# A static decoder-trunk kernel: four first units side by side, zeros on PE at the start, past's loads in a new order, an output projection in three parts, and new costs in the planner

## The chip, the cores and the metric

One core of a Trainium2 chip. The metric is the device time of one execution in microseconds (us); lower is better. The kernel of before took 3124.43 us (median of 3 runs).

## What is computed

One step of a two-layer hybrid decoder for a prompt of 256 rows and a sample group of 8 sequences of 4 rows (288 rows in all), width 2048, in fp32. Cut to what matters here:

```python
for layer in range(2):
    xn = rmsnorm(x, g_mix)
    if layer == 0:                                  # even mixer, phase "m0"
        u, v, q, kvc, kvs, kvw, gl = split(xn @ w_in)
        a = gelu(u) * spatial_gate(rmsnorm(gelu(v)))          # gMLP half
        # NSA half: rows of the past come through a page table (2048 rows per sequence)
        kc, vc = compress(past_cmp ++ new)          # blocks of 64 rows, weighted sums
        o_c, p = cmp_attend(q, kc, vc)              # p ranks the blocks: the 16 best are selected
        o_s = sel_attend(q, top16(p), past_sel ++ new)
        o_w = window_attend(q, past_win ++ new)
        x = x + concat(a, gates(gl) . (o_c, o_s, o_w)) @ w_out
    else:                                           # odd mixer (Mamba-2 SSD), phase "m1"
        x = x + ssd(conv(xn @ w_in), state) @ w_out
    x = x + conv_ffn(rmsnorm(x, g_ffn))             # phases "f0", "f1"
```

Every matrix product `xn @ w` is a projection below. Its weights come from HBM once: 860 tiles of 512 KB.

## The kernel before

**Projections.** TensorE (PE) spends most of its time on them. A unit is 128 output columns over 16 chunks (other counts for some kinds) of 128 inputs. For fp32 accuracy the input is held as `xh + xl` and a weight block as `whi + wlo`; a block of 128x128 is three matmuls with 288 columns: `xh,whi`, `xl,whi`, `xh,wlo` (in the rows: `acc<-xh,whi` and so on). So there are 860 x 8 x 3 = 20,640 projection matmuls. Weights arrive as `wraw` (8 blocks, 5 buffers); a piece is 4 blocks (12 matmuls on PE), for which ScalarE (ACT) writes `whi` (a cast, 128x512) and VectorE (DVE) `wlo` (a subtraction, 128x512), four pieces ahead of PE (`convert`). Positions in the program are counted in pieces below: at 0.1333 us per matmul a piece is 1.6 us of PE. Phase m0 has 212 pieces.

**Order.** All of it is static and fixed when the program is built. `body` walks `all_slots()`, one block after another, and between blocks steps side jobs: Python generators (norms, attention, SSD, loads) that each yield an operation. Whether an operation is put into the program at this point is decided by a planner, `Clock` and `Op`: a cost per engine and element, a hop of 0.2 us between engines, and for PE a margin. A PE operation of a side job is issued when the planner holds its inputs for finished; PE runs in order, so where the real producer is later than planned, PE stands still.

**Start.** `body` issues the input x as four DMAs of four chunks each, weights between them, then page tables and masks (in `enter_m0`). `make_x` writes `xh` (ACT) and `xl` (DVE) of all 16 chunks ahead of the first slot, GpSimd (POOL) squares and adds the even chunks, ACT and DVE the odd ones (`squares`). `make_rstd` sums the squares on PE (`sums`), forms `rstd` on DVE and ACT, and spreads it over the partitions with matmuls on `hl` and `rb`; the first units' results are scaled with it (`h<-acc,rstd`). The first four units (query heads) run one after another, so unit 0 needs all 16 chunks of x within its 16 blocks.

**Past.** `loads` fills a ring `st` of six 512 KB tiles: 64 tiles of compressed rows (`in_ccmp`, gathers by POOL), 8 + 8 of the window (`in_cwk`, `in_cwv`), 32 of selected keys (`in_cselk`; in turn a POOL gather, and four page DMAs on SyncE's queue) and 32 of selected values (`in_cselv`, gathers). `weigh` and `pool_blocks` turn the first 64 into compressed blocks (ACT and DVE weigh, PE sums); `sample` waits for them (flag `pooled`), for the queries and for the gates, then attends: compressed, window, selection of blocks (`rank`), selected keys (`ps<-st,qzr`) and values (`po<-st,PT`).

**Output projection of m0.** `EPARTS` splits its 16 inputs into two parts, chunks 0 to 5 and 6 to 15. Its last unit of part 0 asks for the sample group's attention output (flag `sample`, in `post_e`). With 16 x 10 blocks behind it, that point is piece 172 of 212. `evac_eo` adds a unit's sum of each part to `h`.

All operations of the engines pass one line of the recording layer, L379 in the rows (L391 after the change).

Of the kernel before, what the change touches and what calls it, by code (L numbers as in the profile page):

```python
# [2 lines left out]

# [16 lines left out]
KD = D // 128  # L20
# [5 lines left out]
PIECE, RAW, AHEAD = 4, 8, 4  # L26
EPS = 1e-6
SI, SCV, SH, SG = 4096, 6144, 64, 8
EPARTS = ((0, 6), (6, 16))
# [117 lines left out]
for _n, _w in (("rsel", 256), ("gm", 128), ("cdiag", 128), ("causal", 256), ("newm", 64), ("cadd", 8), ("c01", 8),  # L147
               ("winm", 4), ("vzm", 8), ("hm", 8), ("hmask", 2), ("tle", 128), ("ble", 32), ("i32", 32)):
    EMATS[_n] = (sum(w for _, w in EMATS.values()), _w)
# [4 lines left out]
def even_mats():  # L154
# [19 lines left out]
        i32=np.broadcast_to(t, (128, 32)),  # L174
# [136 lines left out]
class Clock:  # L311


    COST = {"vector": (0.07, 1.04e-3), "scalar": (0.1, 0.834e-3), "gpsimd": (0.147, 2.1e-3)}
    SLOW = {"reciprocal": 6.3e-3, "tensor_tensor_reduce": 0.7e-3}
    TABLES = {AF.Sqrt: 1, AF.Silu: 2, AF.Exp: 3, AF.Tanh: 3}
    HOP = 0.2

    def __init__(self):
        self.free = dict.fromkeys(("tensor", "vector", "scalar", "gpsimd", "sync"), 0.0)  # L320
# [30 lines left out]
class Op:  # L351
# [11 lines left out]
    def start(self):  # L363
# [12 lines left out]
    def run(self):  # L376
# [17 lines left out]
        elif eng == "tensor":  # L394
            n, m = c.width(self.outs[0]), c.width(self.ins[0])
            if self.name == "transpose":
                us = 0.109
# [7 lines left out]
        else:  # L405
# [4 lines left out]
            if eng == "scalar":  # L410
                c0 += 0.05 * ws.count(1)
# [3 lines left out]
            c.free[eng] = end = t + c0 + max(ws) * c.SLOW.get(self.name, c1)  # L415
# [88 lines left out]
class Trunk:  # L504
# [113 lines left out]
    def load_w(self, i):  # L618
        t = yield self.wraw.want([128, RAW, 128], F32, name="wraw")
        self.keep(t)  # L620
        yield self.off.sync.dma_start(t, self.I["w"][i])
# [34 lines left out]
    def body(self):  # L656
# [33 lines left out]
        self.sqs = [self.ssq, self.rstd]  # L690
# [4 lines left out]
        for n in range(KD):  # L695
            self.make_x(n, PHASES[0], n % 2 == 0)
            if n % 4 == 3 and n < AHEAD * PIECE // 2:
                for j in range(n // 4 * AHEAD // 2, (n // 4 + 1) * AHEAD // 2):
                    self.convert(j)
        self.job(self.squares(range(1, KD, 2)), 20.0)  # L700
# [3 lines left out]
        for si, (u, n) in enumerate(slots):  # L704
# [4 lines left out]
            if o == 0:  # L709
                self.convert(j + AHEAD)  # L710
            if n == 0:
# [3 lines left out]
                if free > 2 and (len(u.ks) < 8 or len(pending) >= PMAIN):  # L715
# [74 lines left out]
    def squares(self, ns):  # L790

        nc = self.off
        for i, n in enumerate(ns):
            sq = self.spare[i] if i else self.rstd
            yield nc.scalar.activation(sq, self.h[:, n], AF.Square)
        for i, n in enumerate(ns):
            if i:
                yield nc.vector.tensor_tensor(self.rstd, self.rstd, self.spare[i], op=OP.add)
            self.nsq += 1

    def make_rstd(self):
        nc = self.off
        while self.nsq < KD or self.si < 24:
# [601 lines left out]
    def enter_m0(self, l):  # L1405
# [11 lines left out]
        for n in ("iot", "ptc", "pts", "ptv"):  # L1417
            nc.sync.dma_start(getattr(self, n), I[n])
# [35 lines left out]
        nc.sync.dma_start(self.early, I["emat"][:, :EARLY])  # L1454
# [31 lines left out]
    def even_consts(self):  # L1486

        nc = self.off
        for t, n, c in ((self.ptc, 64, 1), (self.pts, 128, 0), (self.ptv, 32, 2)):
# [278 lines left out]
    def evac_uv(self, u):  # L1768
        nc = self.nc
        if u.half and u.g >= 4:  # L1770
            self.require(("n", u.g - 4 - u.g % 2))
        x = self.w4.tile([128, T], F32, name="x1") if u.half else self.y[:, u.g]
# [70 lines left out]
    def loads(self):  # L1843
# [20 lines left out]
        while self.si < 12:  # L1864
            yield 0.3
        for G in range(2):
            for j in range(8):
                for b in range(4 * G, 4 * G + 4):
                    t = yield from tile()
                    yield gat(t, I["ccmp"], self.ptc[:, 8 * b + j:8 * b + j + 1])  # L1870
                    self.got.append(t)
# [34 lines left out]
    def weigh(self, l, src, dst):  # L1906
# [5 lines left out]
        slots = [x[:, 512 * i:512 * i + 512] for x, n in ((y, 4), (self.S, 3), (self.Sw, 1)) for i in range(n)]  # L1912
        for i in range(64):
            while not src:
                yield 0.3
            t = src.popleft()
            yield [t]
            for h in range(2):
# [3 lines left out]
                else:  # L1922
                    yield nc.vector.scalar_tensor_tensor(slots[i % 8][:, 256 * h:256 * h + 256], a, self.wpq[:, h, 0:1], b,
                                                         op0=OP.mult, op1=OP.add)
            if not l:
                self.rel(t)
                t = slots[i % 8]
            dst.append(t)

    def pool_blocks(self, src):  # L1930

        nc = self.off
        for G in range(2):
            ps = yield self.pside.want([128, 512], F32, name="ps")
            for j in range(8):
                while len(src) < 4:
                    yield 0.3
                yield Burst([self.mm(ps[32 * b:32 * b + 32], self.wpt[:, 28 - 4 * j:60 - 4 * j], src.popleft(),
                                     start=(j == 0), stop=(j == 7)) for b in range(4)])
            yield nc.scalar.copy(self.acc[:, G].rearrange("p h c -> p (h c)"), ps)  # L1940
# [32 lines left out]
    def sample_cmp(self):  # L1973
        nc = self.off
        kct = self.S[:, 256:768].rearrange("p (G h r) -> p G h r", G=2, h=2)
# [45 lines left out]
    def rank(self):  # L2021

        nc = self.off
        v3 = lambda t: t.rearrange("p (n m) -> p n m", n=32)
        a, b = self.S[:, 0:1024], self.S[:, 1024:2048]
        i32 = self.E("i32")
        for G in range(2):
            i_m = self.imp[:, G, None, :].to_broadcast([128, 32, 32])
            i_n = self.imp[:, G, :, None].to_broadcast([128, 32, 32])
            yield nc.vector.tensor_tensor(v3(a), i32[:, :, None].to_broadcast([128, 32, 32]),  # L2030
                                          i32[:, None, :].to_broadcast([128, 32, 32]), op=OP.is_gt)
            yield nc.vector.tensor_tensor(v3(b), i_m, i_n, op=OP.is_equal)
            yield nc.vector.tensor_tensor(b, b, a, op=OP.mult)
            yield nc.vector.tensor_tensor(v3(a), i_m, i_n, op=OP.is_gt)
# [140 lines left out]
```

## Time and profile before

| what | us |
|---|---|
| runs: median, lowest, highest of 3 | 3124.43, 3123.25, 3126.43 |
| the profiled execution's own time | 3120.15 |
| its span, first to last instruction | 3118.4 |
| mean granted TensorE clock | 0.995 |
| PE busy | 3054.7 (98%) |

The rows come from one profiled execution: its span is 1.75 us shorter than its own time, and that time 4.28 us shorter than the median of the runs. PE is busy nearly throughout, so the rows that matter are those of the stretches where it is not, and those where its granted clock (the column PEclk, 1.00 is 2.4 GHz) is below 1. Waits are given with what ended them.

### The profile page before, as it was taken

How to read it: one execution, taken by the hardware profiler on the slowest of the kernel's cores; microseconds unless marked ns; L12 is line 12 of the kernel's file. 1: busy time of each engine (PE TensorE's matmuls, PEld its weight loads, DVE VectorE, ACT ScalarE, POOL GpSimd, SP SyncE). 2: the span in 40 equal slices, each digit the busy share in tenths (PEclk: the TensorE clock that was granted, in tenths of full speed). 3: DMA queues.
4: the chain of work that ended last, by engine and by line, in shares of the span. 5: the costliest groups of instructions: out<-in, count | busy, mean ns of one | idle time of the engine just before them, and what ended most of it. 6: DMA issues, size and time to landing. Idle time of an engine off the chain costs nothing.

```text
span 3118.4 us, 63001 instructions
## 1 busy us (share of the span) xinstructions
PE 3054.7 (98%) x23529; PEld 2953.2 (95%) x23529; DVE 2220.0 (71%) x4575; ACT 1614.9 (52%) x3227; POOL 661.2 (21%) x1044
## 2 busy tenths in 40 slices
PE   7999989999999999999999999999999999999999
PEld 7998879999999999999889988899999999999999
DVE  7987646776577567678889989875677646765764
ACT  6775634554455445555555555554455535544553
POOL 6434443000000000122444445430220000000000
PEclk9999999999999999999999999999999999999999
DMA  7987774444444444555455545565454444444454
GB/s 291 330 314 245 273 271 171 167 163 167 164 164 168 163 164 168 181 187 180 174 184 192 183 161 180 175 208 177 151 176 167 163 167 165 164 168 163 164 179 146
DMA packets 189187, 587.43 MB, mean 188 GB/s; under 512 B 23217, under 2 KB 42961, under 8 KB 188881
## 3 DMA queue, kind: packets, MB, share of 16 engines
q1 hardware_dynamic: 169680, 516.29, 47.7%
q0 software_dynamic: 19200, 67.12, 6.2%
q8 instruction: 185, 3.03, 0.4%
q14 instruction: 122, 0.99, 0.1%
HBM read 555.54 MB, written 27.78 MB: 187 GB/s over the span
## 4 chain that ended last, share of the span: by engine, by line
PE 85%; DVE 6%; DMA 3%; issue 2%; POOL 2%; ACT 2%; SPq 0%; DVEq 0%; ACTq 0%; POOLq 0%
PE acc L379 77%; PE ps L379 7%; DVE wlo L379 2%; DVE cv L379 1%; PE po L379 1%; DMA h<-in_h 1%; DVE h L379 1%; DMA st<-in_cselk,pts 1%; DMA st<-in_cselv,ptv 1%; ACT whi L379 1%; POOL ssq L379 1%; POOL nrm L379 0%; DMA wraw<-in_w 0%; DVE zt L379 0%; DVE cx L379 0%
## 5 line engine op out<-in xcount | busy, mean ns | idle before, releaser
L379 DVE TENSOR_TENSOR wlo<-wraw,whi 128x512 fp32r<-128x512 f32 x1720 | 1232.4, 720 | 781.5 <-ACT whi L379 778.5
L379 ACT CAST whi<-wraw 128x512 fp32r<-128x512 f32 x1720 | 1058.8, 620 | 1090.1 <-PE acc L379 872.7
L379 PE MATMUL acc<-xh,whi 128*128 128x288 f32 x5238 | 1577.2, 301 | 9.4 <-ACT whi L379 8.0
L379 PE MATMUL acc<-xl,whi 128*128 128x288 f32 x5238 | 1549.5, 296 | 3.2 <-DVE xl L379 3.1
L379 PE MATMUL acc<-xh,wlo 128*128 128x288 f32 x5238 | 1544.0, 295 | 1.3 <-DVE wlo L379 1.3
L379 PEld LDWEIGHTS acc<-xh,whi 128*128 128x128 f32 x5238 | 985.9, 188 | 30.0 <-issue 14.2
L379 PEld LDWEIGHTS acc<-xl,whi 128*128 128x128 f32 x5238 | 987.3, 188 | 10.4 <-DVE xl L379 4.8
L379 PEld LDWEIGHTS acc<-xh,wlo 128*128 128x128 f32 x5238 | 989.3, 189 | 1.7 <-DVE wlo L379 1.7
L379 PE MATMUL acc<-hidh,whi 128*128 128x288 f32 x1380 | 407.9, 296 | 0.0
L379 PE MATMUL acc<-hidl,whi 128*128 128x288 f32 x1380 | 407.1, 295 | 0.0
L379 PE MATMUL acc<-hidh,wlo 128*128 128x288 f32 x1380 | 406.1, 294 | 0.0
L379 POOL COPY fcv<-hx 128x18 f32<-128x18 f32 x176 | 36.6, 208 | 1439.8 <-DVE hx L379 1439.8
L379 PEld LDWEIGHTS acc<-hidh,wlo 128*128 128x128 f32 x1380 | 259.8, 188 | 0.0
L379 PEld LDWEIGHTS acc<-hidl,whi 128*128 128x128 f32 x1380 | 259.1, 188 | 0.0
L379 PEld LDWEIGHTS acc<-hidh,whi 128*128 128x128 f32 x1380 | 258.6, 187 | 0.0
L379 DVE SCALAR_TENSOR_TENSOR cv<-hx,prm,cv 128x304 f32<-128x304 f32 x352 | 187.1, 532 | 6.3
L379 DVE SCALAR_TENSOR_TENSOR cv<-cx,sw,cv 128x312 f32<-128x312 f32 x144 | 112.3, 780 | 6.6 <-ACT cv L379 3.2
L379 ACT ACTIVATE cv<-hx,prm 128x304 f32<-128x304 f32 x176 | 112.7, 642 | 0.0
L379 POOL DMA_INDIRECT st<-in_ccmp,ptc x64 | 84.4, 1319 | 94.6 <-DVE S L379 18.1
L379 DVE TENSOR_TENSOR hx<-acc,rstd 128x256 f32<-128x256 f32 x348 | 89.7, 301 | 0.2
L379 POOL TENSOR_TENSOR h<-h,ets 128x512 f32<-128x512 f32 x64 | 78.5, 1250 | 7.4 <-PE po L379 7.3
L379 POOL TENSOR_TENSOR ssq<-ssq,nrm 128x288 f32<-128x288 f32 x76 | 76.3, 1004 | 5.7
(347 smaller groups left out, 2673.3 us busy)
## 6 DMA issues: line engine op xcount, KB each, us to landing
wraw<-in_w SPq DMA_DIRECT2D x860, 512.0 KB
h<-in_h SPq DMA_DIRECT2D x64, 256.0 KB
out_h<-h SPq DMA_DIRECT2D x64, 256.0 KB
st<-in_cselk SPq DMA_DIRECT2D x64, 128.0 KB
st<-in_cwk POOLq DMA_DIRECT2D x8, 512.0 KB, 6.4
st<-in_cwv POOLq DMA_DIRECT2D x8, 512.0 KB, 4.9
h<-in_xT SPq DMA_DIRECT2D x4, 576.0 KB
h<-in_xT SPq DMA_DIRECT2D x16, 144.0 KB
```

The lines of the kernel that those rows point to most:

```text
L379: self.f(*self.args, **self.kw)
```

## The change

1. **Start.** `all_slots` takes the first four units chunk by chunk (block of unit 0, 1, 2, 3 on chunk 0, then on chunk 1). x comes in seven DMAs, the first of one chunk, and the first weight tile in two halves; `first_x` makes a chunk just ahead of its piece. PE first runs 22 matmuls of 128x288 on a zeroed tile. The squares move from POOL to ACT (8 of 128x576) and DVE (7 additions). Page tables and masks are issued at slot 12 (`even_loads`); `make_rstd` starts no sooner than slot 16.
2. **Loads.** The window's 16 tiles and 20 of the compressed ones are interleaved, loads start at slot 20 for 12; `weigh` holds its results in other slots (behind `npool`), and `sample` no longer waits for `pooled` and the gates: `sample_cmp` is a job of its own.
3. **Three parts.** `EPARTS` is (0, 6), (6, 8), (8, 16): the sample group's output is asked for at the end of part 1, and `evac_eo` adds three times.
4. **rank** compares a fourth of the blocks per partition group, on 256 and 512 columns in place of 1024, with one more matmul.
5. **The planner's costs** (`Clock`): POOL 0.147 + 2.1e-3 n becomes 0.3 + 1.9e-3 n; a result is ready 0.08 (DVE), 0.09 (ACT), 0.05 (POOL) after its engine is free; a PE operation on a tile from a DMA is held 1.2 us longer (`LAND`); PE's change of mode is 0.09; a projection matmul is 0.0134 + n/2400 = 0.1334 us for 288 columns, where it was 0.123.

```diff
-EPARTS = ((0, 6), (6, 16))
+EPARTS = ((0, 6), (6, 8), (8, 16))
...
-    for u in all_units():
+    us = all_units()
+    slots, held = [(u, n) for n in range(KD) for u in us[:SIDE]], []
+    for u in us[SIDE:]:
...
-    COST = {"vector": (0.07, 1.04e-3), "scalar": (0.1, 0.834e-3), "gpsimd": (0.147, 2.1e-3)}
-    SLOW = {"reciprocal": 6.3e-3, "tensor_tensor_reduce": 0.7e-3}
+    COST = {"vector": (0.07, 1.04e-3), "scalar": (0.1, 0.834e-3), "gpsimd": (0.3, 1.9e-3)}
+    LAST = {"vector": 0.08, "scalar": 0.09, "gpsimd": 0.05}
+    SLOW = {"reciprocal": 6.3e-3}
...
+    LAND = 1.2
+    TURN = 0.09
...
-                t = max(t, r[4] + (hop if r[6] != me else 0))
+                t = max(t, r[4] + (0 if r[6] == me else hop + (c.LAND if r[6] == "dma" and me == "tensor" else 0)))
...
-                us = 0.003 + n / 2400
+                us = 0.0134 + n / 2400
+            if mode != c.mode:
+                us += c.TURN
...
-            c.free[eng] = end = t + c0 + max(ws) * c.SLOW.get(self.name, c1)
+            c.free[eng] = t + c0 + max(ws) * c.SLOW.get(self.name, c1)
+            end = c.free[eng] + c.LAST[eng]
...
-        for q in range(4):
-            nc.sync.dma_start(self.h[:, 4 * q:4 * q + 4], I["xT"][:, 4 * q:4 * q + 4])
-            if q < 2:
+        for lo, hi in ((0, 1), (1, 2), (2, 4), (4, 6), (6, 8), (8, 12), (12, 16)):
+            nc.sync.dma_start(self.h[:, lo:hi], I["xT"][:, lo:hi])
+            if lo != 1 and self.nraw < 5:
                 self.load_raw()
...
+        for _ in range(IDLE):        # IDLE = 22
+            nc.tensor.matmul(idle, zero[:, :128], zero, start=True, stop=True)
+        for n in range(AHEAD):
+            self.first_x(n)
+            self.convert(n)
...
+            if si == SIDE * 3:
+                nc.sync.dma_start(self.ident, I["ident"])
+                self.even_loads()
...
-        while self.nsq < KD or self.si < 24:
+        while self.nsq < KD or self.si < SIDE * 4:
...
-        while self.si < 12:
+        while self.si < SIDE * 5:
...
+        yield from past(44)
         for G in range(2):
             for k in range(4):
                 t = yield from tile()
                 yield pool.dma_start(t, I["cwk"][G, k])
                 self.got.append(t)
+            yield from past((8, 8)[G])
...
+            yield from past((4, 0)[G])
...
-        yield from self.until("pooled", "q", "gates")
-        self.job(self.sample_cmp())
-        yield from self.until("kw", "vw")
+        yield from self.until("q", "kw", "vw")
...
-        if u.kind == "eo" and u.part == 0 and u.pos > 0 and n == 5:
+        if u.kind == "eo" and u.part < 2 and u.pos > 0 and n == len(u.ks) - 1:
...
-                self.require(("a", 6), ("a", 7), "sample")
+            if end and u.part:
+                self.require("sample")
```

How the order moves, in the three places that matter. ACT at the start, before (`xh` is a chunk of the input, `whi` a piece of weights):

```order
L379 ACTIVATE nrm<-ones 128x1
L379 ACTIVATE xh<-h,prm 128x288 x4
L379 CAST whi<-wraw 128x512 x2
L379 ACTIVATE xh<-h,prm 128x288 x4
L379 CAST whi<-wraw 128x512 x2
L379 ACTIVATE xh<-h,prm 128x288 x8
```

and after the change, from the same instruction on:

```order
L391 ACTIVATE nrm<-ones 128x1
L391 ACTIVATE xh<-h,prm 128x288
L391 CAST whi<-wraw 128x512
L391 ACTIVATE xh<-h,prm 128x288
L391 CAST whi<-wraw 128x512
```

The first piece of weights now stands behind one chunk of x, not four; the squares, 128x576, follow from the fifth chunk on, between later pieces. On PE the sums of squares stand at piece 6.25 before and 17.75 after, and the matmuls that spread `rstd` at 11.5 and 12 before and at 20 after.

POOL's part of the past's loads, before:

```order
L379 DMA st<-in_ccmp,ptc 128x1024 x64
L379 DMA st<-in_cwk 128x1024 x4
L379 DMA st<-in_cwv 128x1024 x4
L379 DMA st<-in_cwk 128x1024 x4
L379 DMA st<-in_cwv 128x1024 x4
L379 DMA st<-in_cselk,pts 128x256 x32
L379 DMA st<-in_cselv,ptv 128x1024 x16
L379 DMA st<-in_cselk,pts 128x256 x32
L379 DMA st<-in_cselv,ptv 128x1024 x16
```

and after:

```order
L391 DMA st<-in_ccmp,ptc 128x1024 x44
L391 DMA st<-in_cwk 128x1024 x4
L391 DMA st<-in_ccmp,ptc 128x1024 x8
L391 DMA st<-in_cwv 128x1024 x4
L391 DMA st<-in_ccmp,ptc 128x1024 x4
L391 DMA st<-in_cwk 128x1024 x4
L391 DMA st<-in_ccmp,ptc 128x1024 x8
L391 DMA st<-in_cwv 128x1024 x4
L391 DMA st<-in_cselk,pts 128x256 x32
L391 DMA st<-in_cselv,ptv 128x1024 x16
L391 DMA st<-in_cselk,pts 128x256 x32
L391 DMA st<-in_cselv,ptv 128x1024 x16
```

The window's tiles stand between the compressed ones; the selected keys and values keep their places at the end. PE first uses a tile of selected keys at piece 117.75 before and 125.5 after.

PE at the end of the sample group's attention, before, with 2,064 projection matmuls (172 pieces) ahead of it:

```order
L379 MATMUL ps<-xh,wlo 128x288
L379 MATMUL po<-st,PT 32x256 x16
L379 MATMUL ps<-ident,S 128x128 x4
L379 MATMUL po<-st,PT 32x256 x16
L379 MATMUL ps<-ident,orow 128x128 x2
L379 MATMUL acc<-xh,whi 128x288
```

The same rows follow one another after the change, with 2,160 projection matmuls (180 pieces) ahead: eight pieces of projection more lie before the last values are needed. Counted over the program, PE has the same projection matmuls, 22 more on zeros and one more in `rank`; DVE 4,577 operations and now 4,595, ACT 3,191 both times, POOL 1,049 and now 1,034. Runs of side work on PE between projection matmuls are 141 in m0 and now 150, in m1 181 and now 213, with as many side matmuls in m1 as before.

## Rows read from the trace of the kernel before

**Rows 1.** Page, part 1: busy time of each engine over the span, its share, and instructions.

```profile
PE 3054.7 (98%) x23529; PEld 2953.2 (95%) x23529; DVE 2220.0 (71%) x4575; ACT 1614.9 (52%) x3227; POOL 661.2 (21%) x1044
```

**Rows 2.** Windows: a stretch of the span (us), its length, the busy time of each engine in it with the instructions, then PE's granted clock, the share of the DMA engines' time, and GB/s.

```profile
core 0: us, PE busy (x) PEld busy (x) DVE busy (x) ACT busy (x) POOL busy (x), PEclk, DMA share, GB/s
0.00:40.00 40.00, 26.76 (x158) 24.64 (x158) 31.15 (x63) 21.55 (x45) 26.68 (x49) 0.91 0.81 287
60.00:80.00 20.00, 16.61 (x116) 14.19 (x115) 14.21 (x36) 10.61 (x24) 12.41 (x11) 0.91 0.91 340
250.00:460.00 210.00, 196.60 (x1981) 172.23 (x1970) 127.64 (x364) 101.88 (x229) 102.54 (x102) 0.97 0.82 277
453.00:461.00 8.00, 5.22 (x31) 1.69 (x29) 0.31 (x1) 0.00 (x0) 0.00 (x0) 0.57 0.34 116
1380.00:2110.00 730.00, 704.68 (x5415) 653.09 (x5414) 631.00 (x1216) 395.52 (x964) 300.83 (x356) 1.00 0.53 181
2000.00:2004.00 4.00, 4.00 (x37) 3.94 (x38) 3.93 (x8) 0.95 (x3) 0.78 (x1) 0.57 0.85 303
2300.00:3118.40 818.40, 814.83 (x6113) 814.59 (x6112) 517.65 (x1019) 393.79 (x674) 28.41 (x167) 1.00 0.48 165
```

**Rows 3.** PE's waits over the whole span: what waited, for which engine and tile; us in total, times, the longest.

```profile
PE acc L379 <- ACT whi L379: 8.0, 1, 8.0
PE ps L379 <- DVE xdd L379: 7.5, 6, 2.1
PE ps L379 <- DMA st<-in_cselk,pts: 6.6, 4, 2.9
PE po L379 <- DMA st<-in_cselv,ptv: 6.1, 5, 2.3
PE po L379 <- DMA h<-in_h: 5.0, 6, 1.4
PE ps L379 <- POOL ssq L379: 4.7, 5, 1.9
PE ps L379 <- DVE mx L379: 3.9, 6, 1.1
PE ps L379 <- ACT ge L379: 3.4, 1, 3.4
PE acc L379 <- DVE xl L379: 3.1, 3, 2.4
PE ps L379 <- ACT ec L379: 2.8, 6, 0.5
PE ps L379 <- DVE hl L379: 2.3, 3, 0.8
```

**Rows 4.** Timeline of PE: start, duration, what ran, how often, and in brackets the idle time before it and what ended that.

```profile
7.97 0.61 PE L379 MATMUL acc<-xh,whi 128*128 128x288 f32 x1 [7.97 <-ACT whi L379]
...
13.41 0.35 PE L379 MATMUL acc<-xh,whi 128*128 128x288 f32 x1
...
18.10 0.61 PE L379 MATMUL acc<-xl,whi 128*128 128x288 f32 x1 [2.45 <-DVE xl L379]
...
18.50 0.44 PE L379 MATMUL acc<-xh,wlo 128*128 128x288 f32 x1
18.74 0.44 PE L379 MATMUL acc<-xh,whi 128*128 128x288 f32 x1
...
27.73 0.25 PE L379 MATMUL ps<-ones,ssq 128*96 128x1 f32 x2
27.84 0.38 PE L379 MATMUL acc<-xh,whi 128*128 128x288 f32 x1
28.05 0.29 PE L379 MATMUL acc<-xl,whi 128*128 128x288 f32 x1
...
70.25 0.67 PE L379 MATMUL ps<-ones,ge 128*96 128x1 f32 x6 [3.39 <-ACT ge L379]
```

**Rows 5.** Timeline of POOL, ACT and DVE at the start, same columns.

```profile
0.76 0.61 POOL L379 MEMSET rb<- 128x288 f32 x2 [0.29 <-POOLq L2162]
...
5.59 1.82 ACT L379 ACTIVATE xh<-h,prm 128x288 fp32r<-128x288 f32 x4 [3.34 <-DMA h<-in_xT]
7.31 1.13 ACT L379 CAST whi<-wraw 128x512 fp32r<-128x512 f32 x2
...
31.76 0.15 DVE L379 TENSOR_SCALAR rms<-ps 96x3 f32<-96x3 f32 x1
...
37.13 0.16 DVE L379 TENSOR_TENSOR hl<-rms,hl 96x3 fp32r<-96x3 f32 x1
...
39.62 0.82 DVE L379 TENSOR_TENSOR h<-acc,rstd 128x288 f32<-128x288 f32 x2
```

**Rows 6.** Timeline of ACT around 63 to 68 us, same columns.

```profile
63.46 0.91 ACT L379 ACTIVATE st<-st,wpq 128x256 f32<-128x256 f32 x2 [2.88 <-DMA st<-in_ccmp,ptc]
...
67.83 0.91 ACT L379 ACTIVATE st<-st,wpq 128x256 f32<-128x256 f32 x2 [2.95 <-DMA st<-in_ccmp,ptc]
```

**Rows 7.** POOL's waits from 20 to 480 us: the ring `st` and who held its tile.

```profile
POOL st L379 <- PE po L379: 74.5, 9, 17.2
```

**Rows 8.** Groups of DVE instructions, the first from the stretch 1380:2110 (m1), the second from 300:1300: operation and shapes xcount, busy time, mean ns of one, idle time before them.

```profile
L379 DVE SCALAR_TENSOR_TENSOR cv<-cx,sw,cv 128x312 f32<-128x312 f32 x144 | 112.3, 780 | 6.6 <-ACT cv L379 3.2
L379 DVE SCALAR_TENSOR_TENSOR cv<-hx,prm,cv 128x304 f32<-128x304 f32 x176 | 93.5, 532 | 3.1
```

More of the change, by code (lines that the diff above doesn't have):

```diff
@@ L2 @@
 from contextlib import ExitStack
+from itertools import islice
 import numpy as np
@@ L694, in body @@
             nc.gpsimd.memset(rb.bitcast(F32), 0.0)
[L695 to L700, printed above, removed]
+        idle = self.pside.give([128, T], F32, name="ps")
+        zero = self.rbs[0].rearrange("p c t -> p (c t)")
+        for _ in range(IDLE):
+            nc.tensor.matmul(idle, zero[:, :128], zero, start=True, stop=True)
+        Slots.back(idle.tensor.name)
+        for n in range(AHEAD):
+            self.first_x(n)
+            self.convert(n)
         pending = deque()
@@ L788, in make_x, with first_x, squares @@
             nc.gpsimd.tensor_tensor(self.ssq, self.ssq, sq, op=OP.add)
-    def squares(self, ns):
-        nc = self.off
[L793 to L799, printed above, removed]
+    def first_x(self, n):
+        self.make_x(n, PHASES[0], False)
+        if n == 1:
+            self.nsq = 0
+            self.job(self.squares(), 4.0)
+    def squares(self):
+        nc = self.off
+        for n in range(0, KD, 2):
+            while self.si < SIDE * (n - 4):
+                yield 0.3
+            sq = self.spare[n % 4 // 2] if n else self.nrm
+            yield nc.scalar.activation(sq, self.h[:, n:n + 2], AF.Square)
+            if n:
+                yield nc.vector.tensor_tensor(self.nrm, self.nrm, sq, op=OP.add)
+            self.nsq += 2
     def make_rstd(self):
         nc = self.off
-        while self.nsq < KD or self.si < 24:
+        while self.nsq < KD or self.si < SIDE * 4:
             yield 0.4
@@ L1488, in even_consts @@
         nc = self.off
+        yield from self.until("loads")
         for t, n, c in ((self.ptc, 64, 1), (self.pts, 128, 0), (self.ptv, 32, 2)):
@@ L1771, in evac_uv @@
             self.require(("n", u.g - 4 - u.g % 2))
+        if not u.half:
+            self.wait(lambda: self.npool >= (64 if u.g > 2 else 32))
         x = self.w4.tile([128, T], F32, name="x1") if u.half else self.y[:, u.g]
@@ L1863, in loads, with past @@
         yield from self.until("rows")
-        while self.si < 12:
+        while self.si < SIDE * 5:
             yield 0.3
[L1866 to L1871, printed above, removed]
+        cmp = iter([(b, j) for G in range(2) for j in range(8) for b in range(4 * G, 4 * G + 4)])
+        def past(n):
+            for b, j in islice(cmp, n):
+                t = yield from tile()
+                yield gat(t, I["ccmp"], self.ptc[:, 8 * b + j:8 * b + j + 1])
+                self.gotc.append(t)
+        yield from past(44)
         for G in range(2):
@@ L1910, in weigh @@
         y = self.y[:, 0:8].rearrange("p k t -> p (k t)")
-        slots = [x[:, 512 * i:512 * i + 512] for x, n in ((y, 4), (self.S, 3), (self.Sw, 1)) for i in range(n)]
+        slots = [x[:, 512 * i:512 * i + 512] for x, ns in ((self.S, (0, 1, 2)), (y, (2, 3, 0, 1))) for i in ns]
         for i in range(64):
-            while not src:
+            ring = slots if i < 32 else slots[:5]
+            while not src or not l and (i >= self.npool + len(ring) or 32 <= i < 37 and self.npool < 32):
                 yield 0.3
@@ L1932, in pool_blocks @@
         nc = self.off
+        yield from self.until("wpt")
         for G in range(2):
@@ L1974, in sample_cmp @@
         nc = self.off
+        yield from self.until("pooled", "q", "gates")
         kct = self.S[:, 256:768].rearrange("p (G h r) -> p G h r", G=2, h=2)
@@ new lines, in rank @@
+        yield nc.vector.tensor_tensor(b, b, e, op=OP.mult)
+        yield nc.vector.tensor_tensor(a, a, b, op=OP.add)
+        yield nc.vector.tensor_reduce(c8, a.rearrange("p (n m) -> p n m", n=16), axis=AX.X, op=OP.add)
+        for o in own(w, lambda G: c8[:, None, 8 * G:8 * G + 8].to_broadcast([128, 4, 8])):
+            yield o
+        ps = yield self.pside.want([128, 64], F32, name="ps")
+        yield self.mm(ps, self.E("gm"), w, start=True, stop=True)
+        yield nc.vector.tensor_scalar(self.selb.rearrange("p G n -> p (G n)"), ps, 14.5, NEG, op0=OP.is_gt, op1=OP.mult)
@@ L2083, in sample_keys @@
         yield nc.vector.reciprocal(st[:, 6:7], st[:, 6:7])
+        yield from self.until("gates")
         yield nc.vector.tensor_tensor(st[:, 6:7], st[:, 6:7], self.grow[:, G, 1 + w:2 + w], op=OP.mult)
@@ L2123, in post_e @@
             self.conv_e(n - 2)
-        if u.kind == "eo" and u.part == 0 and u.pos > 0 and n == 5:
+        if u.kind == "eo" and u.part < 2 and u.pos > 0 and n == len(u.ks) - 1:
+            end = u.pos == KD - 1
+            if end and not u.part:
+                self.require(("a", 6), ("a", 7))
             for k in range(6, 16):
```

98 lines of the change are left out of this document (57 added, 41 removed).

## The prediction, made before the changed kernel was run

> **What bounds the kernel now.** I read the busy times first: PE is busy 3054.7 of 3118.4 us, DVE 71%, ACT 52%, POOL 21% [rows 1]. So PE sets the time, and a change can gain only what PE loses: idle time, half clock, and work beside the projections. The windows show where it loses [rows 2]. In 2300:3118.4, 6,113 matmuls take 814.83 us, 0.1333 us each, with 3.6 us idle: nothing to gain there. Measured with 0.1333, the first 40 us hold 158 matmuls, worth 21.1 us; 18.9 us are lost. 60:80 is idle 3.4 us at clock 0.91. 250:460 is idle 13.4 us at clock 0.97 (another 6.3 us). 1380:2110, the SSD stage, is idle 25.3 us. The waits name the releasers [rows 3]: first weights (8.0), input chunks (3.1), a weighed tile (3.4), selected keys and values (6.6 and 6.1), and, all but a little of it in the SSD stage, xdd, states h, ssq, mx, ec, hl (7.5, 5.0, 4.7, 3.9, 2.8, 2.3: 26.2 together, 32 waits). These eleven lines hold 53.4 of the 63.7 us in which PE is idle. The timeline shows the two prices of a wait: after 2.45 us idle at 18.10, matmuls start 0.24 us apart at 18.50 and 18.74, half clock [rows 4]; such a dip costs 4 x 0.43 = 1.7 us in 2000:2004, at clock 0.57 [rows 2].
>
> The sum below is made against the profiled execution, 3120.15 us; the median of the runs is 4.28 us above it, and that is added at the end. A measurement can tell about 0.2%, 6.2 us, from no change.
>
> **Start: 5.6 us gained.** Before, the first projection waits 7.97 us for whi, since four xh (1.82 us) stand ahead of it on ACT, and the first 576 KB of x land at 5.6 [rows 4, 5]. Projections then run at half clock until 13.41, where the next starts 0.2 us later and the clock rises [rows 4]. After: PE starts its zeros when POOL has cleared rb, 0.76 + 0.61 = 1.4 us [rows 5]; 22 x 0.24 = 5.3 us, so they end at 6.7. Data: even with no earlier landing, one xh (1.82/4 = 0.45) and one cast (0.57) after 5.59 give 6.6. PE was busy 5.4 us before its clock rose (7.97 to 13.41), so the zeros use up that time with nothing lost. One piece of projection then needs only one chunk, and the 2.45 us for xl go. What comes in their place is rstd: sums at piece 17.75 (6.7 + 17.75 x 1.6 = 35.1), and both of its spreading matmuls at piece 20. Between, the chain runs on DVE and ACT with weights between its links; from rms to hl it took 5.4 us (31.76 to 37.13), to the first scaled result 7.9 [rows 5], and 2.25 pieces of cover are 3.6 us. The wait is 1.3 us if DVE is free of queued weights, 5.4 if not. I take 4.5, as hl and rb stand at the same piece and DVE is as full as before, and 1.7 us of half clock behind it. Lost: 6.7 + 4.5 + 1.7 + 0.4 = 13.3 for 18.9. Bounds: -1 (x in seven DMAs lands late and PE waits at each chunk) to +10 (no rstd wait). Squares cost PE nothing: ACT has 8 of 128x576, well under one xh + whi per piece (0.45 + 0.57 of 1.6 us), and POOL's share goes away. Page tables move behind the x DMAs on SyncE's queue; only the gathers need them.
>
> **60:80: 2.5 us gained.** PE's 3.39 us for ge [rows 4] is ACT's: the operations that weigh gathered rows waited 2.88 and 2.95 us for their gathers [rows 6], with weight casts and ge behind them. With the clock of 60:80, 3.4 + 20 x 0.09 = 5.2 us. Loads start at slot 20 and the order of the first 44 tiles is the same; DMA moves 340 GB/s there [rows 2], so the tiles come no faster. But keys and gates no longer meet these tiles at the same piece. I take half, 2.5; bounds 0 and 5.
>
> **Sample group: 6.4 us gained.** Of 250:460 19.7 us are lost, 9 waits for selected keys and values being 12.7 of it, and in 453:461 PE runs 31 instructions at clock 0.57 [rows 2, 3]. Two things move against each other: the end of attention has eight pieces more projection ahead, 96 x 0.1333 = 12.8 us of cover, but the first selected key is used 7.75 pieces, 12.4 us, later. What remains is that the planner now holds each first use of a loaded tile 1.2 us longer: 9 x 1.2 = 10.8, of which I take half, since tiles of the ring follow on one another (a late tile delays the next load: POOL waited 74.5 us for PE to free tiles [rows 7]). 5.4, and 1.0 of clock. Bounds: -8 (453:461 twice) and +16 (all waits and half of the clock's loss). The 16 more additions to h (0.41 us each [rows 5]) and rank lie on DVE beside projections, DVE being 29% idle; without that cover they would cost 6.6 us.
>
> **SSD stage and later: 8.2 us gained.** LAND covers the states' waits (longest 1.4 us, 6 waits, 5.0): 0.4 left. A result latency of 0.08 per DVE operation gives chains of many small operations more room: xdd 7.5 to 4.5, hl 2.3 to 0.5. ssq, mx and ec I leave: their chains stand in the new order much as they did. That is 9.4 us. One of the xdd waits is followed by a window at clock 0.57 for 4 us, 1.7 us lost [rows 2]; it goes nine times in ten if that wait shrinks as I say, 1.5. Against that, 213 insertions of side work for 181: the first projection after one takes 0.21 us to the next start (27.84 to 28.05) for 0.13 [rows 4], 32 x 0.085 = 2.7. 8.2. Bounds: -4 (only the insertions, and one more dip) and +22 (all waits).
>
> **m0's own insertions**, 9 more: -0.8.
>
> Here a rule speaks against the change. cv in the SSD stage takes 780 ns for 128x312, in the FFN 532 for 128x304 [rows 8], and POOL is busy 300.83 of 730 us there, 28.41 of 818.4 in the last stretch [rows 2]; the planner prices both alike, before and after. The Trainium skill, SBUF — State Buffer, section Who interferes with whom, says that a VectorE operation with two SBUF inputs and a GpSimd one that reads SBUF exclude each other. By it the chains that end in xdd and hl would be late by what the planner doesn't hold, and new latencies would not mend it: their 4.8 us would stay, and the sum would be 17.1, 3107, inside the forecast's own range; no row here shows the two engines at the same moment.
>
> Sum: 5.6 + 2.5 + 6.4 + 8.2 - 0.8 = 21.9; 3120.15 - 21.9 = 3098.3, and with 4.28, **3102**.
>
> **Rivals.**
> *A: the past's stream sets the end of the sample group.* The ring has six tiles, and keys are taken 12.4 us later; then the loads slip by as much as the end does, no wait shortens and m0 gains the start alone, partly given back at the gathers. For it: 74.5 us of POOL waiting on PE [rows 7] and DMA at 0.82 in 250:460 [rows 2]. Against it: LAND. With -8 at the sample group, 3102 + 14.4 = 3116; without the gathers' 2.5, 3119.
> *B, slower: the re-measured matmul takes away the planner's room in the SSD stage.* It held a projection matmul for 0.123 us where it takes 0.1333, so each chain had 8% more real time than planned; that is gone, while wide DVE operations, 780 ns for a planned 0.07 + 312 x 1.04e-3 = 0.39 us, stay underpriced. If the stage's 32 waits (26.2 us) double, the stage loses 26.2 + 2.7 where it gained 8.2: 3102 + 37 = 3139. It decides from where the waits' growth eats the other gains: 5.6 + 2.5 + 6.4 - 0.8 - 2.7 = 11.0, 0.34 us more for each wait. Against it: latency, LAND, POOL's higher fixed price, all of which add room. If only m0's gains fall too, 3131 is enough.
> *C: bigger gain.* Both families of waits go, sample group at +16 and the SSD stage at +18: 3102 - 9.6 - 9.8 = 3083, and with the rstd wait at 1.3, 3079; with no gather wait, 3076.
> *D: zeros don't lift the clock*, or hold PE while data are there: another 2.4 us of half clock (5.4 us x 0.44), 3104. That lies within the forecast.
>
> **Chances.** Forecast (3087 to 3115, its own range) 0.62, D within it; C 0.12; A 0.17; B 0.09. A's times straddle 0.2% (3118.2): 0.07 of it counts as faster, 0.10 as the same. Faster 0.62 + 0.12 + 0.07 = 0.81, same 0.10, slower 0.09. Range: below to 3076, C's end; above to 3121, which takes A in; B is left out, and what the bounds add at either end.
>
> **What would show it.** First projection near 6.7 us at clock 1, no wait of PE over 0.5 us at piece boundaries until about 38, then one for hl or rb of 1 to 5 us. In m0, waits for selected tiles of 4 to 8 us in total. In the SSD stage, waits for h under 1, xdd 3 to 6, ssq and mx as now. Wrong: gaps at each chunk of x in the first 30 us, a dip near piece 180, or SSD waits above 26 us.

## The result and the profile after

The changed kernel takes 3153.44 us (median of 4 runs, 3149.89 to 3156.88) beside 3123.84 us of the kernel before (4 runs): a ratio of 1.0098, 95% interval 1.0083 to 1.0112. It is slower by about 30 us where 22 fewer were forecast. Its profiled execution took 3156.88 us, its span is 3154.9 us, its mean clock 0.987.

Where the time went is read by position: between the same projection matmuls (12 to a piece) in both traces. Idle is the sum of PE's gaps, half is the time in which the record of the granted clock shows the lower level (it begins at 13.5 us in the trace of before, at 5.5 in that of after); all in us. The two profiled executions lie 36.7 us apart, the medians 29.6, so the table shows some 7 us more than the change is worth.

| pieces | before | idle, half | after | idle, half | difference |
|---|---|---|---|---|---|
| 0 to 20 | 55.3 | 13.4, 6.8 | 40.2 | 1.6, 0 | -15.1 |
| 20 to 40 | 46.2 | 3.4, 3.4 | 61.6 | 7.9, 23.9 | +15.4 |
| 40 to 212 (end of m0) | 424.6 | 14.6, 13.7 | 439.8 | 24.8, 13.7 | +15.2 |
| 212 to 800 | 961.2 | 2.2, 0 | 954.6 | 0, 0 | -6.6 |
| 800 to 1100 (SSD stage) | 629.0 | 23.9, 3.4 | 659.6 | 41.4, 44.4 | +30.6 |
| rest | 998.4 | 2.7, 3.4 | 996.0 | 1.4, 0 | -2.4 |

The waits of PE, over the whole span of after:

```profile
PE ps L391 <- DVE xdd L391: 15.5, 9, 2.9
PE ps L391 <- POOL ssq L391: 13.3, 7, 2.8
PE po L391 <- DMA st<-in_cselv,ptv: 8.2, 6, 2.2
PE ps L391 <- DVE rb L391: 7.2, 10, 1.0
PE ps L391 <- DVE hl L391: 6.3, 3, 4.8
PE ps L391 <- ACT ge L391: 5.8, 2, 3.7
PE ps L391 <- DMA st<-in_cselk,pts: 3.2, 6, 1.1
```

Against [rows 3] the first weights (8.0) and the states h (5.0) are gone, and xl (3.1) but for 0.5, as forecast. But xdd doubled (7.5 to 15.5), ssq nearly trebled (4.7 to 13.3), hl and rb came up. The windows show the granted clock behind such waits:

```profile
core 0: us, PE busy (x) PEld busy (x) DVE busy (x) ACT busy (x) POOL busy (x), PEclk, DMA share, GB/s
0.00:40.00 40.00, 38.41 (x272) 37.67 (x273) 28.53 (x60) 26.99 (x51) 12.96 (x34) 1.00 0.92 339
40.00:44.00 4.00, 1.16 (x6) 0.62 (x4) 2.36 (x10) 0.62 (x1) 0.00 (x0) 0.88 1.03 420
44.00:60.00 16.00, 15.02 (x70) 14.88 (x70) 5.82 (x19) 7.13 (x13) 0.00 (x0) 0.50 0.16 60
...
470.00:494.00 24.00, 15.76 (x107) 9.88 (x106) 3.73 (x9) 2.60 (x6) 4.68 (x5) 0.86 0.43 151
1380.00:2150.00 770.00, 728.62 (x5528) 683.99 (x5527) 628.17 (x1234) 408.78 (x978) 330.84 (x372) 0.97 0.51 175
```

The first 40 us now hold 272 matmuls, 22 of them zeros, at clock 1.00 (as far as the record goes) for 158 at 0.91 [rows 2]. Then 44:60 runs 70 at clock 0.50, with PE busy 15.02 of 16 us: not idle, slow. In the SSD stage DVE is no busier than before (628.17 us for 631.00 [rows 2]); the order changed. PE's timeline at piece 20:

```profile
6.11 0.29 PE L391 MATMUL acc<-xh,whi 128*128 128x288 f32 x1
...
42.34 0.24 PE L391 MATMUL ps<-ident,hl 96*6 96x96 f32 x1 [1.85 <-issue]
43.56 0.58 PE L391 MATMUL ps<-rb,ones_r 128*128 128x288 f32 x1 [0.98 <-DVE rb L391]
45.12 0.61 PE L391 MATMUL acc<-xh,whi 128*128 128x288 f32 x1 [0.98 <-DVE h L391]
45.52 0.44 PE L391 MATMUL acc<-xl,whi 128*128 128x288 f32 x1
45.77 0.44 PE L391 MATMUL acc<-xh,wlo 128*128 128x288 f32 x1
...
59.85 0.43 PE L391 MATMUL acc<-xh,wlo 128*128 128x288 f32 x1
60.09 0.33 PE L391 MATMUL acc<-xh,whi 128*128 128x288 f32 x1
60.25 0.29 PE L391 MATMUL acc<-xl,whi 128*128 128x288 f32 x1
...
88.17 1.12 PE L391 MATMUL ps<-ones,ge 128*96 128x1 f32 x6 [3.75 <-ACT ge L391]
```

Three waits for rstd, 3.81 us together (the profile names no releaser for the first; DVE writes hl until 42.24), and 17.1 us at half clock (43.1 to 60.1), 0.24 us to the next matmul. The wait for ge is the one of [rows 4] at 70.25, not shorter.

### The profile page after: what moved, and what is told of

Same layout as the page of the kernel before. It is cut to its first block, busy times and chain, and to the rows that moved or that the text cites. A ratio compares the mean times of both kernels' runs of the same rounds, so it can differ in the third digit from the quotient of the medians.

```text
span 3154.9 us, 63177 instructions
## 1 busy us (share of the span) xinstructions
PE 3074.6 (97%) x23553; PEld 2978.9 (94%) x23553; DVE 2181.8 (69%) x4593; ACT 1615.6 (51%) x3227; POOL 705.8 (22%) x1029
## 5 line engine op out<-in xcount | busy, mean ns | idle before, releaser
L391 PE MATMUL acc<-xh,whi 128*128 128x288 f32 x5148 | 1559.0, 303 | 1.0 <-DVE h L391 1.0
L391 PE MATMUL acc<-xl,whi 128*128 128x288 f32 x5148 | 1529.8, 297 | 0.5 <-DVE xl L391 0.5
L391 PE MATMUL acc<-xh,wlo 128*128 128x288 f32 x5148 | 1524.6, 296 | 0.4 <-DVE wlo L391 0.4
L391 PEld LDWEIGHTS acc<-xh,whi 128*128 128x128 f32 x5148 | 976.6, 190 | 17.1 <-issue 9.5
L391 PEld LDWEIGHTS acc<-xh,wlo 128*128 128x128 f32 x5148 | 979.3, 190 | 0.9 <-DVE wlo L391 0.9
L391 PE MATMUL ps<-xh,whi 128*128 128x288 f32 x324 | 98.3, 304 | 0.8 <-ACT xh L391 0.8
L391 PE MATMUL ps<-xh,wlo 128*128 128x288 f32 x324 | 96.3, 297 | 0.7 <-DVE wlo L391 0.7
L391 PE MATMUL ps<-xl,whi 128*128 128x288 f32 x324 | 96.4, 298 | 0.1
L391 DVE SCALAR_TENSOR_TENSOR cv<-cx,sw,cv 128x312 f32<-128x312 f32 x144 | 91.7, 640 | 0.9 <-ACT cv L391 0.6
```

The lines of the kernel that those rows point to most:

```text
L391: self.f(*self.args, **self.kw)
```

## Experiments

"Old costs" are all those of `Clock` and `Op` that the diff changes, put back. The measure of most is the stretch of one profile in which a theory speaks. Such a stretch repeats only roughly once PE waits long in it: two programs with the same order in pieces 800 to 1100 took 659.6 (after) and 651.7 us (a_fill), with 44.4 and 23.9 us of half clock; four with the old costs took 631.0 to 633.8.

| run | median us (runs) | ratio to before, 95% | pieces 20-40 | 40-212 | 800-1100 (idle, half) |
|---|---|---|---|---|---|
| a_pe123 | 3141.72 (5) | 1.0058 (1.0038-1.0078) | 53.4 | 450.7 | 644.0 (30.9, 27.3) |
| a_oldclock | 3117.00 (10) | 0.9984 (0.9974-0.9995) | 51.2 | 433.2 | 631.0 (26.3, 3.4) |
| b_pe133 | 3128.84 (10) | 1.0021 (1.0009-1.0033) | 45.2 | 422.1 | 643.4 (29.6, 17.1) |
| b_newclock | 3145.43 (4) | 1.0077 (1.0056-1.0098) | 46.9 | 418.6 | 660.7 (42.9, 41.0) |
| o_turnland | 3120.97 (1) | | 53.5 | 420.5 | 643.5 (31.9, 20.5) |
| o_last | 3144.14 (1) | | 59.4 | 445.3 | 641.5 (28.4, 20.5) |
| o_pool | 3115.26 (1) | | 51.3 | 431.1 | 631.3 (26.4, 3.4) |
| a_margin | 3135.11 (4) | 1.0052 (1.0035-1.0070) | 47.2 | 441.0 | 646.8 (38.0, 23.9) |
| a_fill | 3143.23 (1) | | 51.7 | 435.9 | 651.7 (41.6, 23.9) |
| s_idle0 | 3121.99 (10) | 0.9993 (0.9982-1.0004) | 45.5 | 438.2 | 633.5 (27.2, 6.8) |
| s_two | 3131.53 (10) | 1.0019 (1.0009-1.0029) | 50.3 | 444.3 | 633.8 (27.9, 3.4) |
| s_loads | 3111.51 (4) | 0.9956 (0.9938-0.9973) | 48.7 | 423.9 | 631.7 (26.1, 3.4) |
| a_wide | 3119.51 (1) | | 46.4 | 434.5 | 640.0 (32.2, 13.7) |
| v_room | 3143.69 (1) | | 59.0 | 443.8 | 642.9 (32.8, 41.0) |
| v_land | 3113.66 (10) | 0.9977 (0.9966-0.9989) | 47.3 | 423.5 | 641.2 (33.7, 27.3) |

**Costs or structure.** Four kernels:

```diff
# a_pe123 (in the changed kernel; b_pe133 the reverse in the kernel before)
-                us = 0.0134 + n / 2400
+                us = 0.003 + n / 2400
# a_oldclock: the changed kernel, every cost of the planner as before
# b_newclock: the kernel before, every cost of the planner as changed
```

> The changed kernel with one cost put back: a projection matmul is 0.003 + n/2400 (0.123 us for 288 columns). Theory 1 (the re-measured matmul took away the planner's room, 8% of each chain's cover): the waits of the SSD stage fall from about 53 to under 32 us and its half-clock stretches from ten to two or three; the time falls by 15 to 30 us, to 3125-3138. Theory 2 (other costs: result latency, landing, mode, POOL): the time stays within 6 us of 3153. Theory 3 (the loads, the three parts and the start, not the costs): within 6 us of 3153 too.

> The changed kernel with all of the planner's costs put back (matmul, POOL, scalar operands, reduce; no result latency, no landing, no mode change): start, loads, three parts and rank remain. Theory 1: as with the matmul's cost alone or a little worse, 3120-3140, SSD stage within 5 us of the kernel before. Theory 2: the SSD stage is back as well, 3120-3140, and better than the matmul alone by over 10 us. Theory 3: still 3145-3160.

> The kernel before with one cost changed: a projection matmul is 0.0134 + n/2400. Theory 1: 15 to 30 us slower than before (3139-3154), the SSD stage alone 15 to 25 us, with waits for xdd, ssq, hl of 40 us or more. Theory 2 and 3: within 6 us of 3124.

> The kernel before with all of the changed kernel's costs, nothing else changed. Theory 1: slower by 10 to 30 us. Theory 2: slower by 10 to 30 us, while the matmul's cost alone is not. Theory 3: within 6 us of 3124. The start is that of before, so the 15 us by which the changed kernel is ahead at piece 20 are missing in any case.

The SSD stage follows the costs and nothing else: 631.0 with the old ones on the new structure, 660.7 with the new ones on the old. Theory 3 falls. The matmul's cost is about half of it: 14.4 us alone (b_pe133), 15.6 of it returned when it is put back (a_pe123). So theory 1 holds there for half, theory 2 for the rest; for the whole time theory 1 gave a_pe123 3125 to 3138 and it took 3141.72, b_pe133 at least 3139 and it took 3128.84. In a_pe123 the waits that stay in the stage are others than in b_pe133: hl 13.0 and rb 6.4 us, xdd 3.7, ssq 2.3, where b_pe133 has xdd 10.7, ssq 5.2, hl 0.6. And a_pe123 lost 10.9 us beside after in pieces 40 to 212 (450.7 for 439.8). Structure alone gains 4 us.

**Which costs.**

```diff
# o_turnland / o_last / o_pool: a_oldclock with
+    LAND = 1.2; TURN = 0.09                               # o_turnland
+    LAST = {"vector": 0.08, "scalar": 0.09, "gpsimd": 0.05}   # o_last
+    "gpsimd": (0.3, 1.9e-3)                               # o_pool
# a_margin: the changed kernel with
-MARGIN = 0.2
+MARGIN = 1.0
```

> The changed kernel with the old costs, and only the landing (1.2 us) and PE's mode change (0.09 us) of the new ones. The measure is the SSD stage's pieces 800 to 1100: 631.0 us with the old costs, 659.6 with the new ones, 15 of the difference being the matmul's price. Theory R (room: what makes the planner's PE slower takes away cover, and a mode change at every insertion does that as the matmul's price does): 641-648, with waits of 30 us or more. Theory L (result latency moves operations to later places): 628-635, and the waits for the states h gone. Theory P (POOL's price): 628-635.

> The changed kernel with the old costs, and only the result latency of the new ones (0.08, 0.09, 0.05 us). Theory R: it adds cover, pieces 800 to 1100 take 622-631 us. Theory L: 641-648. Theory P: 628-635.

> The changed kernel with the old costs, and only POOL's new price. Theory R: 626-633 for pieces 800 to 1100, as POOL's operations are planned a little longer below 750 columns. Theory L: 628-635. Theory P: 641-648, with ssq and POOL's xdd waiting longest.

> The changed kernel, with all its costs, but every PE operation of a side job held 1.0 us after its planned inputs, where it was 0.2. Theory R: the room is back; pieces 800 to 1100 fall from 659.6 to under 635 with under 10 us of half clock, and the whole to 3115-3132. Theories L and P (operations of DVE or POOL stand at bad places in their queues): the waits are not for want of margin, the stage stays above 650 and the whole above 3140.

PE's waits in the SSD stage, in o_turnland:

```profile
PE ps L391 <- POOL ssq L391: 14.3, 7, 2.3
PE ps L391 <- DVE xdd L391: 10.4, 7, 2.3
PE ps L391 <- DVE mx L391: 2.9, 4, 0.7
```

and in o_last:

```profile
PE ps L391 <- DVE hl L391: 12.2, 7, 4.4
PE ps L391 <- DVE rb L391: 6.4, 7, 0.9
...
PE ps L391 <- DVE xdd L391: 2.0, 3, 1.1
PE ps L391 <- POOL ssq L391: 1.4, 2, 1.2
```

Both lose ten or more us, by opposite waits. In o_turnland xdd and ssq come late, as theory R has it: a planned change of mode makes the planner's PE slower. But landing changed with it, and v_land below, with landing and POOL's price and no mode change, loses 9.5 us in the stage (641.2 beside s_loads's 631.7), by xdd too. Which of the two it is stays open. Result latency does what I forecast of it, xdd and ssq nearly go, but seven waits for hl and as many for rb take their place. POOL's price alone does nothing to the stage (631.3). A margin of 1.0 us does as latency does (hl 13.8, rb 6.4, xdd 5.6), so neither R nor its rivals give the 646.8.

**The deadline.** In `evac_z` the fourth z unit of a group asks for the norm of the group before, at piece 24.75 of each 40; its last links are the matmuls on hl and rb. In the program of before the first three groups have hl at 819, 859, 899 and rb 1.5 behind, four pieces ahead of 824.75 and so on. In after hl stands at 823.75, 863.75, 903.75; in o_last, a_margin and a_pe123 at 824.75, 864.75, 904.75. The waits follow these places: of the seven groups in after two have hl at the deadline, 984.75 and 1064.75, and only there PE waits for it (0.91 and 4.78 us); rb stands at the deadline in all seven, and each time PE waits for it.

```diff
# a_wide: the changed kernel with
-            end = c.free[eng] + c.LAST[eng]
+            end = c.free[eng] + (c.LAST[eng] if max(ws) > 12 else 0.0)
# v_room: a_oldclock, past(64), and
-                us = 0.003 + n / 2400
+                us = n / 2400 - 0.007
# v_land: a_oldclock, past(64), LAND = 1.2, "gpsimd": (0.3, 1.9e-3)
```

> The changed kernel, with the result latency for operations on over 12 columns alone, so that the norm's chain on 3 and 6 columns is planned without it (its hl matmul then stands at piece 820.75, not 823.75, its deadline being 824.75). Theory H (deadline): the waits for hl and rb in the SSD stage fall from 12 us or so to under 3, those for xdd and ssq stay near 29, and pieces 800 to 1100 take 645-653 us. Theory R alone (room): taking latency off makes waits longer; 660 or more.

> The changed kernel with the old costs and the old order of loads, and a projection matmul planned at 0.113 us (0.123 before, 0.1334 in the change). Theory R alone: the waits of the SSD stage go on falling, and pieces 800 to 1100 take under 627. Theory H: waits for xdd, ssq and mx nearly go, but the norm's chain stands at its deadline in every group (hl at piece 824.75), with 7 waits for hl and rb of 1 to 5 us; 633-650.

> The changed kernel with the old order of loads and the old costs but for POOL's price and the landing of 1.2 us, without mode change and result latency. Landing adds room where PE waits for the states h (5.9 us with the old costs), and the norm's chain keeps 1 to 3 pieces to its deadline. Theories R and H both: pieces 800 to 1100 take 622-632, the whole 3100-3112. If landing moves the sample group's end as it did not before, up to 3118.

The waits of the SSD stage, in a_wide:

```profile
PE ps L391 <- DVE xdd L391: 12.7, 8, 3.1
PE ps L391 <- POOL ssq L391: 11.9, 7, 2.1
PE ps L391 <- DVE h L391: 5.9, 5, 1.3
```

and in v_room:

```profile
PE ps L391 <- DVE hl L391: 16.6, 7, 6.1
PE ps L391 <- POOL ssq L391: 7.6, 3, 4.1
PE ps L391 <- DVE rb L391: 6.4, 7, 0.9
...
PE ps L391 <- DVE xdd L391: 0.6, 1, 0.6
```

Theory H is borne out from both sides. Taking the latency off the operations of up to 12 columns (by the trace's shapes 64 of 2,224 on DVE, ACT and POOL in this stage, all in the norm's chain) removes hl and rb whole from the SSD stage (640.0 us, below the forecast 645); with more room xdd nearly goes and every group waits for hl (ssq stays in three, against H's letter). In after the first rstd has such a deadline too, at piece 20 (by the code, the next unit's sums need a buffer that only the scaled results free: `acc` in the row at 45.12). In a_wide hl stands at 19.75 and rb at 21.5 (39.64 and 42.54 us), the unit at piece 20 has a side buffer (its rows write `ps`), so there the deadline fell away; PE has no wait for rstd, and pieces 20 to 40 take 46.4 for 61.6 us. In all a_wide takes 3119.51 us in its one run, beside 3120.49 of the kernel before on the same chip. v_land missed in the SSD stage: landing and POOL's price took the states' waits away (5.4 to 1.0), but PE waited 20.4 us for xdd. 13.0 of them are three waits of 4.33 us, each shortly behind a DVE operation of 128x32 that took 6.0 us while POOL ran without a pause (more of this under the rule on ports).

**Clock, loads, parts, zeros.**

```diff
# a_fill: the changed kernel; make_rstd's hl and rb matmuls behind 12 and 7 matmuls on zeros (in each phase)
+        for _ in range(n):
+            yield self.mm(out, zero[:, :128], zero, start=True, stop=True)
# s_idle0, s_two, s_loads: a_oldclock with
-IDLE = 22
+IDLE = 0                                         # s_idle0
-EPARTS = ((0, 6), (6, 8), (8, 16))
+EPARTS = ((0, 6), (6, 16))                       # s_two; post_e, evac_eo as before
-        yield from past(44)
+        yield from past(64)                      # s_loads
```

> The changed kernel with 19 more matmuls on zeros, 12 ahead of the matmul on hl at piece 20 and 7 ahead of that on rb, where PE stood for 1.85 and 0.98 us; they take about as long as PE stood. Theory C (the loss after piece 20 is the clock that falls when PE stands, not work): PE is never idle for over 1 us there, the 17.1 us of half clock from 43.1 on are gone, and pieces 20 to 40 take 52-56 us for 61.6. Rival (PE is slow there because its weights come late: ACT waits and squares fill the engines): half clock or not, pieces 20 to 40 stay at 59-63.

> The changed kernel with the old costs and no matmuls on zeros at the start. Theory C: the first projections run at half clock; 5.4 us of it cost 2.4 us, so piece 20 comes 2 to 6 us later than with zeros (41.1). Rival (the zeros cost as much as they give, PE having to run 22 of them before the first projection): within 1.5 us of 41.1, and the whole within 3 us of 3117.

> The changed kernel with the old costs and the output projection in two parts, so that the sample group's output is wanted at piece 172, not 180. Theory D (the third part gives cover to the sample group): waits at the end grow from 11 us by the eight pieces that are missing, 6 to 12 us slower, 3123-3129. Rival (the sample group's end is set by its own chain of loads and side work, planned anew each time): within 5 us of 3117, since the waits only move.

> The changed kernel with the old costs and the 64 compressed tiles first, the window's 16 after them, as before. Theory E (the new order gives back part of the start's gain: the window's tiles keep the ring from the compressed ones, and selection comes late): pieces 0 to 212 3 to 10 us shorter than 525.6. Rival (the order helps, since the window's attention fills the time of the last loads): 3 to 10 us longer. The end's waits tell: 11.1 us idle in pieces 180 to 212 with the new order.

In a_fill PE runs at piece 20:

```profile
41.08 1.74 PE L391 MATMUL ps<-rb 128*128 128x288 f32 x12
43.06 0.25 PE L391 MATMUL ps<-ident,hl 96*6 96x96 f32 x1 [0.23 <-DVE hl L391]
43.09 1.17 PE L391 MATMUL ps<-rb 128*128 128x288 f32 x7
44.19 0.40 PE L391 MATMUL ps<-rb,ones_r 128*128 128x288 f32 x1
45.57 0.40 PE L391 MATMUL acc<-xh,whi 128*128 128x288 f32 x1 [0.98 <-DVE h L391]
45.81 0.30 PE L391 MATMUL acc<-xl,whi 128*128 128x288 f32 x1
45.94 0.29 PE L391 MATMUL acc<-xh,wlo 128*128 128x288 f32 x1
```

The chain is not sooner done (the first projection behind it starts at 45.57, in after at 45.12), yet the clock holds: 0.13 us to the next matmul, no half clock there, and pieces 20 to 40 take 51.7 us, 9.9 fewer. Half clock in them fell from 23.9 to 3.4 us, an estimated 9.1 us of time (20.5 x (1 - 0.1333/0.24)); the wait for ge fell as well, from 3.75 to 1.4. So most of it was the clock: theory C. Zeros at the start bring piece 20 only 1.3 us sooner (41.1 for 42.4): the rival's side, the first projection starting near 6.2 us with and without. With zeros PE then waits 1.2 us for weights on the way there, without them not at all. The third part is worth 11 us (s_two's ratio of 1.0019 for 0.9984, and 444.3 us for 433.2 in pieces 40 to 212): theory D. The order of loads cost 9.3 us of those pieces, 11.9 of m0 as a whole and 0.0028 of the ratio, 9 us: theory E, and more than its 3 to 10. s_loads is faster than both kernels, 0.9956 (0.9938 to 0.9973) of before.

## Why the prediction was wrong

**What held.** PE bounds the kernel; first projection near 6.7 us at full clock (6.11); the rstd wait, 4.5 us forecast, 3.81 idle; waits for the states h gone; the zeros lifted the clock, so rival D did not come about (they were worth 1.3 us, s_idle0).

**The step that failed** is the term for the SSD stage: "A result latency of 0.08 per DVE operation gives chains of many small operations more room", 8.2 us gained. Measured: 30.6 lost in pieces 800 to 1100, where PE waited 28.8 us for xdd and ssq (10.2 before), 10.5 for hl and rb (2.3), and ran 44.4 us at half clock (3.4). ssq I had put at nothing ("their chains stand in the new order much as they did"); it grew most, from 2.7 to 13.3 in this stretch. The latency alone did shorten xdd, but I had counted on one kind of chain, whose end the planner may hold back, and overlooked the norm, whose end is a deadline; there held links cost. And I held the matmul's price, a rival with 0.09, for a small chance, although front and rows had its whole arithmetic: 0.123 planned for 0.1333 us, and DVE operations of 780 ns planned at 0.39. It was worth 14.4 us alone; mode changes, which I did not count on that side, and landing, which I counted as a gain, 12.5 together. That the old costs' two errors, matmuls and wide DVE operations both planned too short, had offset each other is my reading of this arithmetic: no run prices the DVE operations at what they take. Rival B's 3139 was nearest, its waits doubling (26.2 us forecast to 52): those of xdd and ssq did; mx and ec fell.

**Start and gathers.** "1.7 us of half clock behind it" was sized from one dip [rows 2]; it was 17.1 us long, some 7.6 us (17.1 x (1 - 0.1333/0.24)). The start's 15.1 us up to piece 20 went back there, part by the clock (a_fill) and part as ge's wait stayed (the 3.75 us at 88.17 above, 3.39 in [rows 4]), where I had taken half of it for gone.

**Sample group.** Forecast 6.4 gained; pieces 40 to 212 took 15.2 more. I weighed 12.8 us of cover against 12.4 of delay rightly as opposites: three parts gave 11 (s_two), the loads' order took 9 (s_loads). That order I costed at nothing. PE's waits for selected tiles stayed, 12.9 us for 12.7, where I had forecast 4 to 8. The single costs on the new structure pull apart: landing with mode changes took these pieces from 433.2 (a_oldclock) to 420.5 (o_turnland), with 6.9 us of such waits for 12.5, so my term for landing had the right sign; result latency, which I costed at nothing here, took them to 445.3 (o_last). With all the costs it is 439.8. On the old structure the new costs gained 6.0 (b_newclock, 418.6 for 424.6); why there and not here is open. These are single traces; after and a_fill, with the same order here, differ by 3.9.

**The rule on ports.** By it xdd and hl would have kept their waits, 3107; they did not stay but doubled and more. The Trainium skill, SBUF — State Buffer, section Who interferes with whom, has a VectorE operation with two SBUF inputs contend with a GpSimd one that reads SBUF. The trace of after agrees at the two longest of its nine waits for xdd, 2.84 and 2.87 us. This is the first, on DVE, POOL and PE:

```profile
1913.92 5.65 DVE L391 SCALAR_TENSOR_TENSOR zt<-th,cv 128x256 f32<-128x256 f32 x2 [0.53 <-ACT th L391]
1919.49 0.67 DVE L391 TENSOR_TENSOR xdd<-xdd,ps 128x512 f32<-128x512 f32 x1
...
1914.25 1.29 POOL L391 TENSOR_TENSOR h<-h,ets 128x512 f32<-128x512 f32 x1
1915.51 0.45 POOL L391 TENSOR_TENSOR ec<-ec,zt 128x128 f32<-128x128 f32 x1
1915.91 0.20 POOL L391 COPY cx<-scv 128x24 f32<-128x24 f32 x1
1916.07 1.04 POOL L391 TENSOR_TENSOR h<-h,ets 128x512 f32<-128x512 f32 x1
1917.07 0.45 POOL L391 TENSOR_TENSOR ec<-ec,zt 128x128 f32<-128x128 f32 x1
1917.49 2.03 POOL L391 TENSOR_TENSOR h<-h,ets 128x512 f32<-128x512 f32 x2
...
1920.22 0.67 PE L391 MATMUL ps<-xst,bst 96*128 96x512 f32 x1 [2.84 <-DVE xdd L391]
```

The second operation of the first row, 128x32, took 5.01 us and ended as POOL, after seven operations without a pause, had done; the others of its shape took 0.17 to 1.19 us, in before at most 1.03. It goes the other way too: in three of the seven waits for ssq, an operation of POOL's chain (nrm or y, 128x288) took 2.86 to 3.10 us beside DVE's, at most 1.16 in before. In pieces 800 to 1100 of before and of a_oldclock no DVE operation took over 1.9 us. So part of the growth is the two engines meeting in the order that the new costs make; how much of the 30.6 us it is, no run here tells. The mean of cv, the operation of [rows 8], hides it: 640 ns for 780.

```profile
L391 DVE SCALAR_TENSOR_TENSOR cv<-cx,sw,cv 128x312 f32<-128x312 f32 x144 | 91.7, 640 | 0.9 <-ACT cv L391 0.6
```

## What to carry to other kernels

A static planner's errors may cancel; before one price is made true, ask which other it was paying for, and try each price alone. Sort chains by how they end: where the consumer may be held back, a longer plan is cover, and where a deadline stands behind the chain it is delay, so spare pieces to the deadline are the number to look up in the order. Price a wait on the bounding engine with the slow clock behind it, and fill it if it can't be removed. Where a wait grew, look for a single operation ahead of it far above its usual time: a mean over all of its kind can fall meanwhile.

## What the runs showed of the hardware

The time at half clock behind a wait was much longer than I had expected: 17.1 us behind 3.81 us of waits at piece 20 in after, though PE was busy 15.02 of 16 us in 44:60. In pieces 800 to 1100 of after ten stretches of half clock, 3.4 or 6.8 us each, stand at ten of its eleven longest waits; in a_fill, with the same order there, six stand at six of the thirteen longest. So the same waits do not always bring it. At the end of s_two's sample group, where PE waited 14 times within 42 us, the lower level held for 30.7 us:

```profile
425.00:475.00 50.00, 32.66 (x211) 15.34 (x210) 5.78 (x17) 6.27 (x10) 14.34 (x15) 0.62 0.56 204
```

With matmuls on zeros in two of the three waits at piece 20 the record has no half clock there (a_fill).

DVE and POOL shut each other out for microseconds: a two-input DVE operation of 128x32 took 5.01 us in after and 6.0 in v_land while POOL ran seven or eight operations without a pause, and ended with them.
